# Softmax normalisation moved: attention probabilities multiplied by 1/z on GpSimd ahead of their transposes, in a new order of all mixer operations

## The chip, the core and the metric

The kernel runs on one NeuronCore of a Trainium2 chip. A core has a matrix engine (TensorE, PE in the profile, with its weight loads as PEld), a vector engine (VectorE, DVE), an activation engine (ScalarE, ACT), GpSimd (POOL) and a queue engine (SyncE, SP) that here only starts transfers. The metric is the device time of one execution in microseconds, lower is better.

## What is computed

One layer of an encoder on 512 tokens of width 1024 in float32: a half-step feed-forward network (SwiGLU, inner width 2752), a mixer with two parallel head groups, a second half-step feed-forward network, and a last norm. Cut to what matters here:

```
x = x + 1/2 * SwiGLU_1(RMSNorm(x))
h = RMSNorm(x);  u = h @ w_in            # [ fourier 512 | q 8x64 | k 2x64 | v 2x64 ]
A = FourierMixer(u[:, :512])
q = rope(rms_norm(q)); k = rope(rms_norm(k))
scores = (q . k) / 8                     # each of 8 query heads against its key-value head
p = softmax(scores)                      # exp(s - max) / z,  z = sum of exp over the 512 keys
B = p @ v
x = x + concat([A, B]) @ w_out
x = x + 1/2 * SwiGLU_2(RMSNorm(x))
y = RMSNorm(x)
```

The change concerns the division by z.

## The kernel before

**Tiles and precision.** Activations lie transposed: width on the 128 partitions, the 512 tokens along the free axis. Every product in float32 precision is made of three matmuls on a high part and a low part of each operand (high with high, high with low, low with high). High parts are copies on ScalarE or DVE, low parts are `lows` (line 126, a subtraction on DVE). Weights come from HBM into a raw tile of 512 KB; there are three such tiles (line 89), and a weight's load, its high part and its low part are the operations `.r`, `.h` and `.l`.

**The mixer's operations and their order.** All work of the mixer is cut into named operations. The text `ORDER` (line 47) lists them, and a loop at line 1315 issues them under a manual schedule: each of the five engines executes its own operations in exactly this order, and waits on semaphores for data of the others. Work of the two feed-forward networks on DVE and ScalarE is placed around the mixer's operations by the scheduler at build time; there only PE and SP are in the order of the program (line 120). The names that the prediction uses:

- `wk`, `wq0` to `wq3`, `wv`, `f0` to `f3`, `fw`, `o0` to `o7`: weights; `k.0` to `k.7`, `q0.0` and so on: the eight product steps of a projection.
- `n1.c`, `n1.m`, `n1.p`: the norm ahead of the mixer. `k.sq`, `k.pq`, `k.s0`, `k.s1` (line 900, a power on POOL): the norm of the key heads, likewise for q. `cos`: the loads of the cosine and sine tables. `k.rc`, `k.rs`: the rotation, one and two steps on DVE. `kw`, `kp`, `km`: the keys' norm factors widened, transposed on PE, and multiplied in. `pos`: three tables for the Fourier mixer, loaded from POOL's queue.
- Attention is worked in eight blocks (t, b), t from 0 to 3, b 0 or 1, one query head each. In a block, for each of four groups c of 128 queries: `s` (scores, two matmuls into a PSUM bank, line 1142), `m` (maximum on DVE, line 1148, and its scaling, line 1149), `e` (exponential on ScalarE, which also writes the sum z of its 512 keys). Then for each group kc of 128 keys: `t` (four transposes, one from each of the four query groups, line 1168), `h` and `l` (high and low part), `v` (two matmuls with the values, line 1211, added up over kc). `o..c` and `o..a` collect the two halves of the result.
- `z0.r`, `z0.w`, `z0.p`, `r0.m`: 1/z of both heads of one t, widened to 64 columns on POOL, transposed into rows on PE (line 1200), and multiplied into the collected result (line 1232). `r0.h`, `r0.l` split it for the output projection.
- `map`, `d`, `c`: the Fourier mixer. `y0.0` to `y7.7`: the output projection; `.x` adds the residual, `.h` and `.l` make the operands of the second network's first product, `.q` and `.a` square and accumulate for its norm.

The exponentials lie in a pool of nine tiles (line 763). The eight PSUM banks go around in the order of the list.

**After the mixer** the second network opens with a gate product of eight steps that reads the operands of all eight y; ahead of its last step stand the matmuls for the sums of squares.

Of the kernel before, what the change touches and what calls it, by code (L numbers as in the profile page):

```python
# [6 lines left out]
F32 = mybir.dt.float32  # L7
# [14 lines left out]
HD = 64  # L22
# [30 lines left out]
q1.s1 e001 q2.2 m011 vp q2.3 q1.ah q2.4 s010 f0.r f2.r q1.al q3.1 q2.5 q2.6 e003 q2.7 f0.h q3.2 n1.p m010  # L53
q2.sw s012 q3.3 f0.l f1.h t000 e010 q2.sd e011 q2.rc m012 t003 vs q2.sq h000 fw.r t001 s013 e012 s102 t002
f1.l m102 q3.4 v.h q3.5 h002 q3.6 f00.0 l000 s100 m013 h001 l002 v.l l001 e013 e102 q3.7 q2.pq f2.h m100 v000
q3.sw z0.r q3.sd t010 q2.s0 q1.bh q2.s1 v001 q2.rs f01.0 e100 f2.l s101 f00.1 q2.ah h010 m101 q3.sq f02.0
q1.bl l010 o2.r s103 v002 e101 f02.1 h003 t011 q3.rc q2.bh f00.u l003 h011 m103 q2.bl v003 t013 f02.e e103
t012 o0.r q3.rs q3.pq s112 v010 q3.ah l011 f01.1 q2.al s110 q3.s0 h012 h013 s113 l012 v011 o00.c o00.a l013
m113 m112 s212 e113 m110 f03.0 f01.u e112 m212 q3.al o1.r t103 f03.1 f3.h t101 h101 v012 q3.s1 h103 f03.e
l101 v013 e212 t100 h100 o01.c f10.0 f3.l l103 fw.h s213 l100 q3.bh f12.0 o01.a s111 f03.h f10.1 f02.h q3.bl  # L60
t102 f10.u f03.l e110 s210 s211 h102 v100 m213 z0.w e213 f02.l m111 v101 e111 s201 m210 m211 f12.1 o5.r l102
f12.e e211 z0.p r0.m t111 t112 v102 h111 h112 fw.l l112 v103 o10.c s203 f12.h e210 t110 f11.0 h110 m201 l111
# [6 lines left out]
d3.h c0.l m313 c2.c h300 v202 e313 c1.l v203 y0.0 o20.c m310 h301 l300 c2.o y0.1 e310 d3.l l301 o20.a z2.w
z3.r y1.0 y1.1 c2.h t303 v300 o2.h c3.s c3.c t310 v301 c3.q o7.r t302 c2.l y1.2 h310 h303 c3.o h302 y0.2 l302  # L70
t312 z2.p c3.h v302 c3.l t311 h311 l310 l303 y1.3 y1.4 o6.r z3.w r1.h l311 t313 v310 y0.3 h313 o2.l v303
o30.c r1.l y2.0 y1.5 v311 y2.1 h312 l313 l312 r2.m v312 v313 z3.p o30.a y2.2 y0.4 r2.h o31.c r2.l o31.a y1.6
y0.5 r3.m y0.6 r3.h y2.3 r3.l y0.7 y2.4 o3.h y2.5 y2.6 o3.l y1.7 y2.7 y1.x y3.0 o5.h o5.l y3.1 y3.2 y2.x y0.x
y3.3 y2.q o4.h y5.0 y3.4 o4.l y3.5 y5.1 y0.q y1.q y3.6 y5.2 y5.3 y3.7 y5.4 y5.5 y4.0 y5.6 y4.1 y3.x y4.2 o6.h
# [11 lines left out]
def encoder(ctx, tc, A, out):  # L86
    nc = tc.nc
# [659 lines left out]
    with tc.tile_pool(name="mix", bufs=1) as mp, tc.tile_pool(name="mixt", bufs=1) as mt:  # L747
# [384 lines left out]
        prob, parts, pts, outs, pair, zs, zps, sps, mxs = {}, {}, {}, {}, {}, {}, {}, {}, {}  # L1132
# [50 lines left out]
        def sum_ops(t):  # L1183


            @op(f"z{t}.r")
            def _():
                nc.vector.reciprocal(zs[t], zs[t])

            @op(f"z{t}.w")  # L1190
            def _():
                zw = tp.tile([P, 4, 2, HD], F32, tag="wide", bufs=1, name=f"zw{t}")
                nc.gpsimd.tensor_copy(zw, zs[t].unsqueeze(3).to_broadcast([P, 4, 2, HD]))
                zs[t] = zw

            @op(f"z{t}.p")
            def _():
                zps[t] = bank_for(f"z{t}")
                for c in range(4):
                    nc.tensor.transpose(zps[t][:, c * P : (c + 1) * P], zs[t][:, c].rearrange("p a b -> p (a b)"), ident)  # L1200
# [347 lines left out]
```

## Time and profile before

| | us |
|---|---|
| runs | 824.57, 826.18, 826.47 |
| median of the runs | 826.18 |
| span of the profiled execution, first to last instruction | 821.1 |
| median less span | 5.1 |
| PE busy in the span | 814.0 |
| DVE busy | 640.8 |
| ScalarE busy | 464.5 |
| GpSimd busy | 30.6 |

The profile is of one execution, and gives its span alone; the share of a run ahead of and behind the span is worked out from the median. "L1200" is line 1200 of the kernel. A row "x16" is a group of 16 instructions; in rows of the order in time the first two numbers are start and duration in us, and a bracket gives the idle time before and what ended it. Matmuls overlap: one takes longer from start to end than the distance to the next one's start. TensorE ran at its full granted clock, 1.000.

### The profile page before, as it was taken

Reading aid. Unit: us, or ns where it says so; the run is one execution under the profiler, and the core shown is the slowest. Engines: PE = TensorE matmul, PEld = TensorE weight load, DVE = VectorE, ACT = ScalarE, POOL = GpSimd, SP = SyncE. Lnnn points to the kernel's source line nnn. Section 1 sums busy time; section 2 is a strip of 40 time slices with the busy share of each in tenths; the row PEclk is TensorE's granted clock in tenths of the full one; section 3 lists DMA queues with packets and bytes.
Section 4 is the critical chain, followed back from the end, with each engine's and each line's share of the span. In section 5 each row is a group of like instructions: output and inputs, shape, how many; then the busy total and the mean of one; then the engine's idle time right before and its main releaser. Section 6 shows DMA issues by size and latency. Waiting matters only on the chain.

```text
span 821.1 us, 13621 instructions
## 1 busy us (share of the span) xinstructions
PE 814.0 (99%) x5378; PEld 747.0 (91%) x5378; DVE 640.8 (78%) x996; ACT 464.5 (57%) x777; POOL 30.6 (4%) x34
## 2 busy tenths in 40 slices
PE   9999999999999999999999999999999999999997
PEld 7889999899989998889998888899989999899986
DVE  7998896489756947799998488998945896479574
ACT  7764664167524635676886358556632673256462
POOL 0110000000000000222000000100000000000001
PEclk9999999999999999999999999999999999999999
DMA  7664322323242213621110233552232322322222
GB/s 257 182 145 174 123 91 78 123 103 141 66 153 89 74 58 116 225 77 52 52 52 27 87 105 105 123 170 112 93 121 112 126 103 69 131 104 97 69 78 103
DMA packets 31168, 89.58 MB, mean 109 GB/s; under 512 B 3712, under 2 KB 8832, under 8 KB 31104
## 3 DMA queue, kind: packets, MB, share of 16 engines
q1 hardware_dynamic: 27776, 82.61, 28.9%
q0 software_dynamic: 2608, 5.12, 3.3%
q10 hardware_dynamic: 720, 0.98, 0.3%
q8 instruction: 42, 0.69, 0.3%
q14 instruction: 22, 0.18, 0.1%
HBM read 84.24 MB, written 2.10 MB: 105 GB/s over the span
## 4 chain that ended last, share of the span: by engine, by line
PE 97%; DVE 1%; issue 1%; DMA 0%; ACT 0%; POOLq 0%; POOL 0%; DVEq 0%
PE dn L183 25%; PE r L419 23%; PE q L419 12%; PE mix L183 9%; PE gu L183 8%; PE p L419 6%; PE gu L708 3%; PE mix L1211 2%; PE mix L1168 2%; PE mix L1142 1%; PE mix L1006 1%; PE mix L1008 1%; PE mix L1007 1%; PE mix L1143 1%; PE mix L1065 1%
## 5 line engine op out<-in xcount | busy, mean ns | idle before, releaser
L419 PE MATMUL r<-rt,ring 128*128 128x256 f32 x1686 | 209.3, 276 | 0.0
L183 PE MATMUL dn<-at,ring 128*128 128x512 f32 x900 | 203.3, 380 | 0.5 <-DVE ring L127 0.4
L419 PEld LDWEIGHTS r<-rt,ring 128*128 128x128 f32 x1686 | 200.4, 188 | 0.8
L183 PEld LDWEIGHTS dn<-at,ring 128*128 128x128 f32 x900 | 168.1, 188 | 29.8 <-DVE ring L127 1.6
L419 PE MATMUL q<-rt,ring 128*128 128x256 f32 x840 | 106.6, 276 | 0.0
L127 DVE TENSOR_TENSOR ring<-s,ring 128x1024 fp32r<-128x1024 f32 x70 | 85.6, 1223 | 24.0 <-ACT ring L378 20.8
L419 PEld LDWEIGHTS q<-rt,ring 128*128 128x128 f32 x840 | 100.4, 188 | 0.0
L543 DVE SCALAR_TENSOR_TENSOR gx<-dn,gx 128x512 f32<-128x512 f32 x61 | 42.0, 690 | 67.6 <-PE dn L183 67.6
L378 ACT CAST ring<-s 128x1024 fp32r<-128x1024 f32 x70 | 73.5, 1050 | 28.0 <-PE p L419 13.6
L169 ACT CAST ring<-raw_dn 128x768 fp32r<-128x768 f32 (+3 forms) x58 | 45.2, 783 | 71.1 <-PE dn L183 62.2
L127 DVE TENSOR_TENSOR ring<-raw_dn,ring 128x768 fp32r<-128x768 f32 (+3 forms) x58 | 51.6, 893 | 5.7 <-PE r L419 4.4
L419 PE MATMUL p<-rt,ring 128*128 128x256 f32 x420 | 53.3, 276 | 0.0
L127 DVE TENSOR_TENSOR ring<-raw_g,ring 128x1024 fp32r<-128x1024 f32 x35 | 42.8, 1221 | 11.1 <-PE p L419 10.2
L419 PEld LDWEIGHTS p<-rt,ring 128*128 128x128 f32 x420 | 50.2, 188 | 0.0
L183 PE MATMUL gu<-ring 128*128 128x512 f32 x216 | 48.9, 381 | 0.0
L183 PEld LDWEIGHTS gu<-ring 128*128 128x128 f32 x216 | 40.4, 188 | 6.9
L378 ACT CAST ring<-raw_g 128x1024 fp32r<-128x1024 f32 x35 | 36.8, 1051 | 15.8 <-DMA raw_g<-in_wgu 8.5
L427 ACT COPY p<-r 128x256 f32<-128x256 f32 x35 | 13.0, 371 | 46.8 <-PE r L419 46.5
L451 ACT ACTIVATE g<-g 128x512 f32<-128x512 f32 x35 | 22.1, 633 | 23.4 <-DVE g L450 23.1
L387 ACT CAST ring<-raw_u 128x512 fp32r<-128x512 f32 x35 | 21.8, 624 | 17.4 <-PE q L419 15.9
L183 PE MATMUL mix<-near,ring 128*128 128x512 f32 x120 | 29.7, 383 | 0.0
L464 DVE TENSOR_TENSOR u<-g,u 128x512 f32<-128x512 f32 x35 | 24.1, 689 | 6.1 <-ACT u L463 6.0
(269 smaller groups left out, 1300.5 us busy)
## 6 DMA issues: line engine op xcount, KB each, us to landing
raw_g<-in_wgu SPq DMA_DIRECT2D x35, 512.0 KB, 3.6
raw_u<-in_wgu SPq DMA_DIRECT2D x35, 512.0 KB, 4.4
raw_dn<-in_wd SPq DMA_DIRECT2D x40, 384.0 KB, 3.1
raw_gu<-in_wgu SPq DMA_DIRECT2D x12, 512.0 KB, 3.7
raw_o<-in_wo SPq DMA_DIRECT2D x8, 512.0 KB, 3.5
raw_dn<-in_wd SPq DMA_DIRECT2D x8, 448.0 KB, 3.4
raw_wq<-in_wins SPq DMA_DIRECT2D x4, 512.0 KB, 3.6
raw_f<-in_winf SPq DMA_DIRECT2D x4, 512.0 KB, 4.5
```

The source lines that it names most:

```text
L127: nc.vector.tensor_tensor(out=lo, in0=src, in1=asf(hi), op=ALU.subtract)
L169: nc.scalar.copy(hi[:, :n, :], raw[:, :n, :])
L183: nc.tensor.matmul(ps, a, b, start=first and b is mhi and a is whi, stop=last and a is wlo)
L378: nc.scalar.copy(hi, src)
L387: nc.scalar.copy(hi, src)
L419: nc.tensor.matmul(ps[:, t], a[:, ks], b[:, i, t], start=first and i == 0 and o == 0, stop=i == KH - 1 and o == 2, skip_group_check=not first,
L451: nc.scalar.activation(b["g"], b["g"], AF.Silu)
L464: nc.vector.tensor_tensor(out=u, in0=b["g"], in1=u, op=ALU.mult)
L543: nc.vector.scalar_tensor_tensor(out=x[d][:, t], in0=ps[:, t], scalar=0.5, in1=x[d][:, t], op0=ALU.mult, op1=ALU.add)
L708: nc.tensor.matmul(turned(pss[c]), w[:, k % 2, c], turned(m[k]), start=k == 0 and m is hh and w is hi, stop=k == KD - 1 and w is lo,)
L1168: nc.tensor.transpose(pts[n][:, c * P : (c + 1) * P], prob[t, b, c][:, kc * P : (kc + 1) * P], ident)
L1211: nc.tensor.matmul(turned(outs[t, b]), w, turned(p), start=kc == 0 and i == 0, stop=kc == 3 and i == 1)
```

## The change

1/z is no longer multiplied into the result. `z..` now takes the reciprocal of one head's sums (four per row, of one block), and `p..`, one for each query group, multiplies the 512 probabilities of each query in place by its 1/z on GpSimd. The transposes read the product. The widening on GpSimd, the sixteen transposes of 1/z on PE with their PSUM banks, and the multiplication of the result on DVE are gone. The list of operations is a new one from end to end; of it the parts are shown that the prediction speaks of.

```diff
 ORDER = """
-wq0.r wk.r wv.r wk.h pos wq0.h wk.l k.0 k.1 k.2 k.3 wq1.r k.4 wq1.h k.5 k.6 k.7 wv.h n1.c k.sq wq0.l q0.0
-q0.1 q0.2 cos k.pq wq1.l n1.m q0.3 q0.4 k.sw f3.r q0.5 wv.l wq2.r k.s0 q0.6 k.s1 k.rc q0.7 q1.0 wq2.h k.rs
-q1.1 q1.2 q1.3 q0.rc q0.sq kw f1.r wq2.l kp v.0 q0.sw km k0.2 q0.pq k0.0 k1.0 q0.s0 v.1 q1.4 q0.rs k1.3 q1.5
-v.2 wq3.r k0.1 v.3 q0.bh q1.6 k0.3 q1.7 q2.0 q0.ah q1.sq q0.al s000 v.4 q0.bl v.5 wq3.h s001 s002 s003 q0.s1
-v.6 k1.1 m000 k1.2 q1.sw wq3.l q1.sd q2.1 e000 m002 m003 q1.rc m001 q1.pq e002 v.7 q1.s0 q1.rs vt q3.0 s011
...
-e300 e311 h203 d20 v213 o21.c s303 d21 c0.o h201 l200 t202 v200 o3.r m303 s312 l203 c1.c z2.r e303 o21.a c1.s
-d30 c0.h d2.h l201 c1.q z1.p t300 m312 v201 d2.l c1.o d31 c2.s h202 e312 r1.m s310 l202 s313 c2.q c1.h t301
...
-y1.h y4.3 y2.h y5.7 y4.4 o6.l y4.5 o7.h y5.x y0.h y6.0 y5.h y4.6 y3.h y1.l y1.a o7.l y3.q y6.1 y2.l y5.q y4.7
-y7.0 y4.x y4.q y3.l y7.1 y6.2 y2.a y7.2 y4.h y6.3 y5.l y6.4 y6.5 y3.a y0.l y7.3 y6.6 y6.7 y4.a y5.a y7.4 y6.x
-y4.l y7.5 y6.h y6.l y6.q y7.6 y7.7 y7.x y6.a y7.q y7.h y7.a y7.l
+wk.r wk.h wq0.r wk.l wq0.h k.0 wq1.r wv.r wq2.r wq1.h k.1 k.2 k.3 k.4 k.5 k.6 wq0.l n1.c wq1.l wq3.r k.7 k.sq
+q0.0 n1.m k.sw q0.1 wq2.h k.pq q0.2 cos q0.3 q0.4 q0.5 k.s0 q0.6 k.s1 k.rc k.rs kw q0.7 q1.0 wq2.l wv.h kp q0.sw
+km k1.2 k0.0 k1.0 q0.rc wv.l q1.1 q0.rs q1.2 f1.r q0.ah q2.0 q1.3 q1.4 k0.3 q1.5 k1.3 q0.al q2.1 k0.1 q0.sq q2.2
+k0.2 q2.3 q0.bh q1.6 q1.7 q0.pq wq3.h q1.sq k1.1 q1.sw v.0 s000 v.1 s001 f0.r s002 q0.bl q0.s0 s003 q1.pq wq3.l
+q2.4 q0.s1 q1.rc q2.5 q1.s0 m002 q3.0 m003 s012 q2.6 e003 m000 n1.p m001 q2.7 q3.1 e000 s010 s013 q1.sd q1.rs
+e002 f0.h q3.2 m012 e001 s011 v.2 q1.ah v.3 m010 v.4 f0.l q3.3 z00 m011 q1.al v.5 p001 v.6 q1.bh q2.sw v.7 q2.sq
+q1.bl p000 q2.pq f1.h vt q3.4 p003 e010 p002 m013 vp e011 q3.5 vs s101 t001 q3.6 t003 q1.s1 e012 pos t000 s100
...
+l203 v200 s310 p300 v201 c1.h c2.s m310 v202 c2.q m313 c1.l t300 t302 c2.c e310 h302 e313 y2.0 v203 y2.1 c3.s
+t301 c2.o c3.q h300 o0.l z31 p310 h301 t303 l300 c2.h y0.0 l301 p313 y0.1 v300 l302 c3.c p312 h303 r1.h p311
+c3.o v301 c2.l v302 t310 c3.h h310 o20.c l303 t312 r0.l c3.l r1.l o1.l y0.2 y2.2 t311 h311 v303 h312 y2.3 o30.c
...
+o4.l y0.x y3.2 y3.3 o5.h y3.4 y4.0 y2.x y1.x y1.h y4.1 y0.q y4.2 y3.5 o5.l y3.6 y1.l y0.h y4.3 y3.7 y4.4 y4.5
+o7.h o7.l y0.l y4.6 y5.0 y5.1 y5.2 y1.q y2.q y7.0 y7.1 y3.x y7.2 y5.3 y5.4 y4.7 y5.5 o6.h y2.h y4.x y7.3 y1.a
+y3.q o6.l y5.6 y7.4 y5.7 y2.l y4.q y4.h y2.a y6.0 y7.5 y3.a y7.6 y7.7 y6.1 y6.2 y7.x y4.l y7.h y6.3 y5.x y6.4
+y6.5 y6.6 y3.h y5.h y3.l y5.l y4.a y6.7 y6.x y5.q y7.l y5.a y6.h y6.q y6.l y6.a y7.q y7.a
 """
...
@@ -1129,7 +1129,7 @@
             op(f"c{g}.l")(lambda: lows(ml[g], fos[g, 1], mh[g]))
 
 
-        prob, parts, pts, outs, pair, zs, zps, sps, mxs = {}, {}, {}, {}, {}, {}, {}, {}, {}
+        prob, parts, pts, outs, pair, zs, sps, mxs = {}, {}, {}, {}, {}, {}, {}, {}
 
         def score_ops(t, b, c):
             n = f"{t}{b}{c}"
@@ -1183,21 +1183,18 @@
         def sum_ops(t):
 
 
-            @op(f"z{t}.r")
-            def _():
-                nc.vector.reciprocal(zs[t], zs[t])
-
-            @op(f"z{t}.w")
-            def _():
-                zw = tp.tile([P, 4, 2, HD], F32, tag="wide", bufs=1, name=f"zw{t}")
-                nc.gpsimd.tensor_copy(zw, zs[t].unsqueeze(3).to_broadcast([P, 4, 2, HD]))
-                zs[t] = zw
-
-            @op(f"z{t}.p")
-            def _():
-                zps[t] = bank_for(f"z{t}")
+            for b in range(2):
+
+                @op(f"z{t}{b}")
+                def _(b=b):
+                    nc.vector.reciprocal(zs[t][:, :, b], zs[t][:, :, b])
+
                 for c in range(4):
-                    nc.tensor.transpose(zps[t][:, c * P : (c + 1) * P], zs[t][:, c].rearrange("p a b -> p (a b)"), ident)
+
+                    @op(f"p{t}{b}{c}")
+                    def _(b=b, c=c):
+                        e = prob[t, b, c]
+                        nc.gpsimd.tensor_scalar(out=e, in0=e, scalar1=zs[t][:, c, b : b + 1], scalar2=None, op0=ALU.mult)
 
         def attended_ops(t, b, kc):
             n = f"{t}{b}{kc}"
@@ -1227,11 +1224,6 @@
                 read(f"o{t}{b}")
 
         def result_ops(t):
-            @op(f"r{t}.m")
-            def _():
-                nc.vector.tensor_tensor(out=pair[t], in0=zps[t], in1=pair[t], op=ALU.mult)
-                read(f"z{t}")
-
             op(f"r{t}.h")(lambda: nc.scalar.copy(qa[t], pair[t]))
             op(f"r{t}.l")(lambda: lows(qb[t], pair[t], qa[t]))
 
```

More of the change, by code (lines that the diff above doesn't have):

```diff
@@ L53 @@
[L53 to L62, printed above, removed]
@@ L68 @@
-d30 c0.h d2.h l201 c1.q z1.p t300 m312 v201 d2.l c1.o d31 c2.s h202 e312 r1.m s310 l202 s313 c2.q c1.h t301
[L69 to L72, printed above, removed]
@@ new lines @@
+h113 p213 p210 e201 map1 l113 o4.r m203 e202 v112 f13.e p212 s301 t210 v113 map0 o0.h map1.h d00 e203 t211 m301
+map1.l o11.c e301 d01 o11.a h210 h211 o10.a s302 map0.h l210 f13.h t213 t212 map0.l o6.r d0.h h213 d10 m302 z20
+p200 l211 v210 h212 s303 d11 d0.l s300 l213 c0.s p203 s311 l212 d1.h c0.q p201 e302 p202 v211 d1.l m300 e300
+m303 t201 t202 v212 t200 c0.c m311 f13.l e303 s312 m312 v213 d20 e311 h202 c0.o z30 c1.c h201 r0.h d21 o3.r l201
+d30 c1.s l202 p302 c0.h d2.h h200 c0.l l200 p303 d31 c1.q d3.h o1.h c1.o d2.l s313 d3.l t203 o7.r p301 h203 e312
```

17 lines of the change are left out of this document (11 added, 6 removed).

## The prediction

> **What bounds the kernel now.** I read the page first (busy times, chain), then what TensorE (PE) waited for, then the stretches of the mixer, and last the order in time at three places of it.
>
> ```profile
> span 821.1 us, 13621 instructions
> PE 814.0 (99%) x5378; PEld 747.0 (91%) x5378; DVE 640.8 (78%) x996; ACT 464.5 (57%) x777; POOL 30.6 (4%) x34
> PE 97%; DVE 1%; issue 1%; DMA 0%; ACT 0%; POOLq 0%; POOL 0%; DVEq 0%
> ```
> ```profile
> PE dn L183 <- DVE ring L127: 0.4, 1, 0.4
> 366.00:447.00 81.00, 81.00 (x562) 74.36 (x561) 76.72 (x152) 63.22 (x130) 6.16 (x6) 1.00 0.14 49
> ```
>
> PE is the chain for 97%, its largest wait inside the program is 0.4 us, and that one lies in a feed-forward stage (dn), not in the mixer. The second row of the second fence is the attention stretch, 366 to 447 us, with busy time of PE, weight loads, VectorE (DVE), ScalarE, GpSimd (POOL): PE 81.00 of 81.00, DVE 76.72, POOL 6.16, granted clock 1.00. So the mixer's length is what PE issues. Work that other engines gain or lose costs nothing until PE waits for it. DVE, with 4.3 us free in 81, is the engine that comes next.
>
> **Removed, and what it saves.** Four times: a reciprocal of all eight sums, the widening copy on POOL, four transposes of 1/z, and the multiplication of the result on DVE.
>
> ```profile
> L1200 PE MATMUL mix<-ident,zw x16: 269/272/273, 402.3 to 451.9; 128*128 128x128 f32 x16
> L1188 DVE RECIPROCAL z<-z x4: 182/195/197, 373.6 to 440.2; 128x8 f32<-128x8 f32 x4
> L1232 DVE TENSOR_TENSOR oo<-mix,oo x4: 680/684/691, 403.6 to 453.2; 128x512 f32<-128x512 f32 x4
> L1193 POOL COPY zw<-z x4: 609/614/617, 388.5 to 444.3; 128x512 f32<-128x512 f32 x4
> 344.89 0.60 PE L942 MATMUL mix<-ident,kw 128*128 128x128 f32 x4
> 345.25 0.92 PE L183 MATMUL mix<-ring 128*128 128x512 f32 x3
> ```
>
> A transpose takes 272 ns, but they are pipelined: the next product starts 345.25 - 344.89 = 0.36 us after a set of four began. Four such sets: 1.44 us of PE's issue, and as PE had no idle time in the mixer, all of it is on the path. This is the whole gain that the removal can bring. DVE loses 4 x (0.195 + 0.684) = 3.5 us and gets eight smaller reciprocals, at most 8 x 0.195 = 1.6 us; ScalarE keeps its work. Neither is on the path.
>
> **Added: 32 multiplications on POOL, 128x512, in place.** No row shows one. Nearest rows: the copy above, same shape, 0.61 us; and the two-input multiplication at half the length:
>
> ```profile
> L1334 POOL TENSOR_TENSOR gx<-gx,rb x2: 732/733/734, 810.5 to 811.1; 128x256 f32<-128x256 f32 x2
> ```
>
> Lower bound 0.61; upper bound twice 0.733 = 1.47. The new instruction streams one tensor, like the copy, and has a per-partition factor besides, so I take 0.8. In total 32 x 0.8 = 26 us, which POOL has free; what counts is the time from a block's last score to its first transpose, since a transpose of any 128 keys needs all four products of the block, and 1/z needs all four exponentials.
>
> That time is covered by what the new order gives PE between the two. Prices of PE steps: a full 128x512 product of three matmuls 4.64/21 x 3 = 0.66 (the 21 matmuls below), four transposes 0.36, three 256-column matmuls 0.35, the two matmuls of an attended step 0.54:
>
> ```profile
> 412.45 0.28 PE L1006 MATMUL mix<-ring 128*128 128x256 f32 x1
> 412.80 0.28 PE L1006 MATMUL mix<-ring 128*128 128x256 f32 x1
> 414.20 0.48 PE L1211 MATMUL mix<-ph,near 128*128 128x512 f32 x1
> 414.74 0.40 PE L185 MATMUL mix<-ring,chan 128*128 128x512 f32 x1
> 486.42 4.79 PE L183 MATMUL gu<-ring 128*128 128x512 f32 x21
> 491.06 0.95 PE L241 MATMUL ss<-ones,acc 128*128 128x2 f32 x8
> ```
>
> Counted for all eight blocks, the tightest in the new order is the last, (3,1): between s310 and t310 stand six v, four c, four t and four y steps: 6 x 0.54 + 4 x 0.35 + 4 x 0.36 + 4 x 0.66 = 8.7 us. In the old order the tightest was (3,0): two d halves (six 256-column matmuls each, 0.70), one v, one score (two 512-column matmuls, 0.44), two c, and one set of transposes each for t202 and z1.p: 1.40 + 0.54 + 0.44 + 0.70 + 0.72 = 3.8 us, in which maximum and exponential were done with no wait on PE. That leaves (3,1) 8.7 - 3.8 - 0.2 for the reciprocal = 4.7 us, four multiplications of 1.17 us. But z31 stands on DVE, which executes in order, behind m310, m313, c1.l, c2.o and o0.l:
>
> ```profile
> L1148 DVE TENSOR_REDUCE mx<-mix 128x1 f32<-128x512 f32 x26 | 17.8, 684 | 0.3 <-PE mix L1143 0.2
> L1149 DVE TENSOR_TENSOR mx<-mx,sc 128x1 f32<-128x1 f32 x26 | 4.2, 160 | 1.0
> L127 DVE TENSOR_TENSOR pl<-mix,ph 128x512 fp32r<-128x512 f32 x30 | 20.3, 684 | 1.8 <-ACT ph L1173 1.8
> ```
>
> Two maxima of 0.84, a low of 0.68, c2.o at most like o0.l, a conversion of 1.22, and the reciprocal: 5.0 us, if nothing older is left over. 8.7 - 5.0 = 3.7, a limit of 0.92; an older conversion in the way would make it 0.6. At 0.8 I take the cover to hold: 0 us, and 4 x 0.1 = 0.4 us for every 0.1 us above the limit. The other seven covers, counted in the same way, are 11 us and more, with more score work in them. The multiplications themselves delay on POOL only the head powers of q1 to q3 and n1.p.
>
> **Moved: the constants.** The cosine and sine loads now stand on SP behind wq3, which waits for wq1's raw buffer.
>
> ```profile
> 330.95 0.33 SPq L1291 DMA_DIRECT2D cos<-in_cos  x1
> 331.33 0.43 SPq L1292 DMA_DIRECT2D sin<-in_sin  x1
> 334.22 1.22 DVE L127 TENSOR_TENSOR more<-raw_wq,more 128x1024 fp32r<-128x1024 f32 x1
> cos<-in_cos SPq DMA_DIRECT2D x1, 256.0 KB, 5.0
> raw_fw<-in_fw SPq DMA_DIRECT2D x1, 256.0 KB, 4.3
> 338.48 0.60 PE L889 MATMUL mix<-ident,sq_k 128*128 128x128 f32 x4
> 340.42 0.75 DVE L871 SCALAR_TENSOR_TENSOR rot_k<-mix,qkg,cos 128x512 f32<-128x512 f32 x1 [0.41 <-ACT sw_k L854]
> 342.44 0.75 DVE L871 SCALAR_TENSOR_TENSOR rot_q<-mix,qkg,cos 128x512 f32<-128x512 f32 x1
> 343.11 0.42 DVE L933 TENSOR_SCALAR kw<-sc 128x512 f32<-128x512 f32 x1
> ```
>
> The conversion of wq1 ends at 335.44; then wq3, then cos at about 335.8 (SP steps are 0.38 apart), landing at 340.1 (4.3, as fw) to 340.8 (5.0). k.rc and k.rs take 342.44 - 340.42 = 2.02, kw 0.42, so kw is ready at 342.5 to 343.3. PE reaches kp earlier than before: k.pq goes from third to second place behind q0's products (338.48 - 0.66 = 337.8), and kp follows after 0.36 + 7 x 0.66 = 5.0, at 342.8. Wait 0 to 0.5 us; I take 0.3. The three position tables (POOL's queue) move from the mixer's start to behind the first four multiplications; their first reader is map1, late in the order: 0.
>
> **Moved: the end.** The old order ends with y7, the new one with y6, after more finishing work.
>
> ```profile
> 486.62 0.69 DVE L1254 TENSOR_TENSOR gx<-mix,gx 128x512 f32<-128x512 f32 x1 [0.40 <-PE mix L183]
> 487.23 0.68 DVE L1265 TENSOR_TENSOR acc<-acc,sq 128x512 f32<-128x512 f32 x1
> 487.83 1.22 DVE L127 TENSOR_TENSOR ring<-raw_gu,ring 128x1024 fp32r<-128x1024 f32 x1
> 488.96 1.22 DVE L127 TENSOR_TENSOR at<-raw_gu,at 128x1024 fp32r<-128x1024 f32 x1
> 490.10 0.69 DVE L1265 TENSOR_TENSOR acc<-acc,sq 128x512 f32<-128x512 f32 x1
> 490.70 0.74 DVE L213 SCALAR_TENSOR_TENSOR ring<-gx,ring 128x512 fp32r<-128x512 f32 x1
> ```
>
> The gate product starts at 486.42 and its 21st matmul is followed at 491.06, 4.64 us later, by the sums of squares; the last accumulation ended at 490.79, 0.27 us early. Behind the last product DVE had two operations, two conversions of gate weights that went ahead (1.13 each), then the accumulation. New: y6.x, y7.l, y5.a, y6.l, y6.a, y7.a, with steps of 0.61, 0.69, 0.61, 0.69, 0.61, 0.69: 3.90, from 0.20 behind the last product to 4.10. With both conversions ahead as now: 6.36, so PE waits 1.7 us; with one 0.6; with none 0. I take 1.1, between one and both. What else is late by it: the row of the norm, which follows the sums and moves along with PE.
>
> **Sum.** -1.44 + 0 + 0.3 + 1.1 = 0.0 us on a span of 821.1. The runs' median is 826.18, 5.1 above the span; I leave that share as it is: 826.1. Its own range is 824.7 (both moved places free) to 827.7 (0.5 and 1.7, and 0.8 at the blocks).
>
> **A port of SBUF.** The head powers on POOL, 128x8 each, show that it does not run independently of DVE:
>
> ```profile
> 347.62 2.02 POOL L900 TENSOR_TENSOR sc<-sc,mhalf 128x8 f32<-128x8 f32 x1 [5.85 <-DVE sc L896]
> 348.18 0.69 DVE L878 TENSOR_TENSOR rot_q<-rot_q,sw_q 128x512 f32<-128x512 f32 x1
> 386.87 1.64 POOL L900 TENSOR_TENSOR sc<-sc,mhalf 128x8 f32<-128x8 f32 x1 [9.85 <-DVE sc L896]
> 387.31 0.67 DVE L1226 TENSOR_TENSOR oo<-mix,oo 64x512 f32<-64x512 f32 x1
> ```
>
> Beside a DVE operation with both inputs in SBUF (rot_q, sw_q) the power takes 2.02; beside one with an input from PSUM (mix) 1.64. DVE's 0.69 is not longer there. The Trainium skill, page "SBUF — State Buffer", section "Who interferes with whom", says that the two share a port pair as an exclusive lock, and that whichever comes second waits for the whole instruction; the POOL rows agree in direction, and no row shows DVE waiting. By that rule the sum is that of rival (2).
>
> **Rivals.** (1) All covers hold: -1.44, 824.7. For it: the products that need the two conversions at the end come 5 us later, so these could stand back; against: the rows show both ahead. (2) DVE is held up by POOL: 26 us of multiplications in some 81 are a third of the time. DVE's stretch holds 26 tiny scalings of maxima (two SBUF inputs) and, since maxima (17.8) and lows of PSUM tiles (20.3) make half of the 76.7 us, an estimated 25 other two-input operations among the rest. Of these 51 a third meets a running multiplication and waits half of 0.8: 51/3 x 0.4 = 6.8 us. DVE has 4.3 free plus 1.9 saved. It decides from the point where DVE's loss passes these 6.2 at a block's edge; PE would pay between 0 and 6.8, say 3: 829.1. For it: DVE is 95% busy; against: its rows beside POOL are not longer. (3) The multiplication takes 1.2 us or more: 4 x 0.4 = 1.6 at (3,1), and with three more blocks half exposed 3 x 0.8 = 2.4: 830.1. It decides from about 1.1. (4) More than the transposes goes, over 2.5 us in all: no row of the mixer shows it; 823.6.
>
> **Chances.** Forecast 0.45, (1) 0.2, (2) 0.15, (3) 0.15, (4) 0.05. A difference under 0.3%, 2.5 us, can't be told from none. Faster by more: 0.05, case (4). Slower: (2) and (3), 0.30. Within: 0.65. The range takes in (1) and most of (2) and (3): 824.2 to 829.8.
>
> **What would show it.** No L1200 rows and 32 POOL multiplications near 0.8 us; PE idle before kp up to 0.5 us and before the sums of squares up to 1.7; no wait of a transpose (L1168) for POOL. Rows of two-input DVE operations clearly over 0.69 speak for (2), POOL rows over 1.1 for (3). A time below 823.7 or above 828.7 makes the forecast wrong.

## The result: slower by 1.7%

The changed kernel takes 839.56 us (median of 4 runs, 839.31 to 841.83) beside 826.33 us for the kernel before. The ratio is 1.0171, with a 95% interval of 1.0148 to 1.0195: slower by some 14 us. The forecast of 826.1 us is wrong, and so is its range. (Most kernels' runs lie in two groups about 2.2 us apart, mostly 824 to 825.5 and 826.5 to 828 for the kernel before; the ratios below are of all runs, so where 1 us matters the means of the lower groups are given too, 839.5 for the change and 824.7 for the kernel before.)

The profile after, first the page's head and the chain's line, then PE's waits (in all, times, longest), then the attention stretch with the columns of the prediction:

```profile
span 837.7 us, 13615 instructions
PE 817.4 (98%) x5362; PEld 745.9 (89%) x5362; DVE 640.5 (76%) x996; ACT 464.6 (55%) x777; POOL 79.1 (9%) x62
PE 83%; DVE 8%; POOL 5%; issue 3%; ACT 1%; DMA 0%; DVEq 0%; POOLq 0%
```
```profile
PE mix L1168 <- POOL e L1197: 9.1, 7, 2.4
PE dn L183 <- DVE ring L127: 1.5, 2, 0.9
PE mix L1142 <- ACT e L1156: 1.0, 1, 1.0
PE gu L183 <- DVE ring L213: 0.8, 1, 0.8
...
PE ss L241 <- DVE acc L1257: 0.7, 1, 0.7
```
```profile
366.00:447.00 81.00, 74.25 (x498) 66.70 (x497) 68.58 (x135) 56.93 (x117) 51.65 (x34) 0.98 0.21 68
```

Before, PE was busy for 81.00 of these 81 us and DVE was next with 76.72. Now PE is busy for 74.25 us, POOL for 51.65, and the longest entry among PE's waits is the one that the prediction said would not be there: the transposes of the probabilities (L1168) wait for the multiplications on POOL (L1197). The view of that one line says why (durations in ns: minimum, median, maximum):

```profile
L1197 POOL TENSOR_SCALAR e<-e,z x32: 1554/1567/2399, 365.4 to 454.1; 128x512 f32<-128x512 f32 x32
```

A multiplication takes 1.57 us, not 0.8, and up to 2.4. Four of them, one behind the other, take 6.3 us and more, against a cover that the prediction put at 3.7 us at the tightest block. The timeline at another block, (1,1), shows PE's wait, twice 1.21 us, and the instruction behind each gap:

```profile
404.02 5.15 POOL L1197 TENSOR_SCALAR e<-e,z 128x512 f32<-128x512 f32 x3
...
406.20 0.27 PE L1168 MATMUL mix<-ident,e 128*128 128x128 f32 x1
...
407.68 0.33 PE L1168 MATMUL mix<-ident,e 128*128 128x128 f32 x1 [1.21 <-POOL e L1197]
...
409.22 0.88 PE L1168 MATMUL mix<-ident,e 128*128 128x128 f32 x6 [1.21 <-POOL e L1197]
```

Two more things are in the profile. DVE operations with both inputs in SBUF are longer while POOL multiplies (the grouped rows stand with the experiments). And the wait above is followed by a stretch in which TensorE had half its clock. Four neighbouring windows of 3.41 us (sum of PE, PE's weight loads, DVE, ACT, POOL; granted clock):

```profile
403.26:406.67 3.41, 3.21 (x23) 2.69 (x21) 3.34 (x8) 3.33 (x8) 3.41 (x3) 1.00 0.00 0
406.67:410.08 3.41, 1.19 (x9) 1.00 (x10) 3.30 (x7) 1.89 (x5) 3.41 (x3) 1.00 0.00 0
410.08:413.49 3.41, 3.41 (x17) 3.11 (x16) 0.94 (x3) 0.20 (x1) 2.92 (x3) 0.50 0.02 5
413.49:416.90 3.41, 3.41 (x26) 3.20 (x25) 1.69 (x3) 2.60 (x5) 3.41 (x3) 1.00 0.00 0
```

In the second window PE was busy for 1.19 of 3.41 us. In the third it was busy throughout, at a clock of 0.50, and got through 17 matmuls where the fourth has 26: about half the window, 1.7 us, is lost. So by this estimate a wait of 2.4 us cost some 4 here.

### The profile page after: what moved, and what is told of

Same layout as the page of the kernel before. It is cut to its first block, busy times and chain, and to the rows that moved or that the text cites. A ratio compares the mean times of both kernels' runs of the same rounds, so it can differ in the third digit from the quotient of the medians.

```text
span 837.7 us, 13615 instructions
## 1 busy us (share of the span) xinstructions
PE 817.4 (98%) x5362; PEld 745.9 (89%) x5362; DVE 640.5 (76%) x996; ACT 464.6 (55%) x777; POOL 79.1 (9%) x62
## 4 chain that ended last, share of the span: by engine, by line
PE 83%; DVE 8%; POOL 5%; issue 3%; ACT 1%; DMA 0%; DVEq 0%; POOLq 0%
PE dn L183 24%; PE r L419 23%; PE q L419 11%; PE gu L183 7%; PE mix L183 6%; PE p L419 6%; POOL e L1197 4%; PE gu L708 3%; DVE ring L127 1%; DVE mx L1148 1%; DVE pl L127 1%; PE mix L1168 1%; DVE near L127 1%; DMA raw_first<-in_first 0%; PE last L533 0%
## 5 line engine op out<-in xcount | busy, mean ns | idle before, releaser
L183 PE MATMUL dn<-at,ring 128*128 128x512 f32 x900 | 203.5, 381 | 1.5 <-DVE ring L127 1.5
L183 PEld LDWEIGHTS dn<-at,ring 128*128 128x128 f32 x900 | 168.0, 188 | 31.1 <-DVE ring L127 2.8
L1197 POOL TENSOR_SCALAR e<-e,z 128x512 f32<-128x512 f32 x32 | 51.9, 1637 | 38.9 <-DVE z L1190 38.9
L183 PE MATMUL gu<-ring 128*128 128x512 f32 x216 | 49.2, 382 | 0.8 <-DVE ring L213 0.8
L183 PEld LDWEIGHTS gu<-ring 128*128 128x128 f32 x216 | 40.3, 188 | 8.0 <-DVE ring L213 1.2
L255 POOL TENSOR_TENSOR r<-ms,mhalf 128x4 f32<-128x4 f32 (+1 forms) x4 | 4.3, 1068 | 368.9 <-DVE ms L248 368.9
L900 POOL TENSOR_TENSOR sc<-sc,mhalf 128x8 f32<-128x8 f32 x5 | 9.2, 1847 | 305.4 <-DVE sc L896 305.4
```

Of the source, the lines that this page charges most:

```text
L183: nc.tensor.matmul(ps, a, b, start=first and b is mhi and a is whi, stop=last and a is wlo)
L900: nc.gpsimd.tensor_tensor(out=v, in0=v, in1=mhalf.rearrange("p (c t) -> p c t", t=2), op=ALU.pow)
L1197: nc.gpsimd.tensor_scalar(out=e, in0=e, scalar1=zs[t][:, c, b : b + 1], scalar2=None, op0=ALU.mult)
```

## The experiments

Theories: (A) the price of a multiplication, through the chain of four in front of the transposes; (B) the port, POOL and DVE slowing each other; (C) the new order, whatever normalises. The figures of all kernels first; the ratio is to the kernel before on the same chip, and "no 1/z" means that the result is not divided by the sums.

| kernel | what it is | median us (runs) | ratio [95%] |
|---|---|---|---|
| the change | | 839.56 (4) | 1.0171 [1.0148, 1.0195] |
| e1_no_mult | multiplications out, no 1/z | 826.52 (10) | 1.0016 [1.0003, 1.0028] |
| e2_half | on 256 of 512 columns | 827.6 (10) | 1.0026 [1.0012, 1.0039] |
| e3_pow | chain without streaming, no 1/z | 834.48 (4) | 1.0104 [1.0080, 1.0129] |
| e4_dve | multiplications on DVE | 836.27 (4) | 1.0131 [1.0113, 1.0149] |
| e5_tt | POOL, two-input form | 832.86 (4) | 1.0086 [1.0067, 1.0104] |
| e6_tail | e1, other end, no 1/z | 825.3 (12) | 1.0008 [0.9998, 1.0019] |
| e7_oldz, e13_oldz2 | old normalisation, new order | 830.21 (5), 831.2 (6) | 1.0068 [1.0054, 1.0082], 1.0064 [1.0049, 1.0079] |
| e8_split | half POOL, half ScalarE, end as e6 | 829.49 (5) | 1.0059 [1.0046, 1.0073] |
| e9_stream | streaming without chain, no 1/z | 831.05 (5) | 1.0070 [1.0057, 1.0084] |
| e10_order, e15_order2 | e6, order mended twice, no 1/z | 825.36 (12), 825.3 (12) | 1.0003 [0.9993, 1.0014], 1.0003 [0.9991, 1.0015] |
| e11_mixed | e10, multiplications on three engines | 829.68 (5) | 1.0049 [1.0036, 1.0061] |
| e12_none | old order, no 1/z | 821.9 (6) | 0.9962 [0.9947, 0.9976] |
| e14_oldz3 | old normalisation, new order | 830.24 (6) | 1.0065 [1.0048, 1.0083] |

**Is it the multiplications at all?** e1 takes them out and leaves the order; e2 multiplies half of the columns (the other half is not divided).

```diff
                         e = prob[t, b, c]
-                        nc.gpsimd.tensor_scalar(out=e, in0=e, scalar1=zs[t][:, c, b : b + 1], scalar2=None, op0=ALU.mult)
+                        # e1: nothing here; e2: the same instruction behind  e = e[:, : S // 2]
```

> The new order with the 32 multiplications left out (the result is not divided by z). Theory A (price: the multiplication on GpSimd takes 1.55 us alone, 6.2 us for the four of a block, and PE waits for that at the transposes): the waits of PE at line 1168, 10.4 us, and the stretch of half clock behind two of them, about 1.7 us, go; the waits of the new order that have nothing to do with them, 1.6 us between 352 and 362 us and 1.9 us ahead of the sums of squares, stay: 839.6 - 12.1 = 827.5 us. Theory C (the new order itself is slow, on any engine): 835 us or more.

> Each multiplication on 256 of the 512 columns (the other half of the probabilities is not divided by z), about 0.8 us each, which is the price that the prediction assumed. A: waits at the transposes all but go, 828 us, within 1 us of the kernel without multiplications. If the price is per instruction and not per column, or if the port decides (theory B: GpSimd and DVE hold each other up), the rows stay near 1.5 us and the time stays above 835.

Without them, 13 of the 14 us are gone (1.0171 / 1.0016 = 1.0155, 12.8 us; 14.0 between the lower groups, 839.5 and 825.5). At half the columns an instruction takes 0.93 us, near the forecast's 0.8, and the covers do hold: one wait of 0.4 us for POOL is left on PE, at block (3,1).

```profile
L1198 POOL TENSOR_SCALAR e<-e,z x32: 915/927/1712, 365.3 to 442.6; 128x256 f32<-128x256 f32 x32
PE mix L1168 <- POOL e L1198: 0.4, 1, 0.4
```

So at about the price that the prediction took there is next to no wait. What the covers hold at 1.57 us is another question, answered further down.

**Chain or port?** e3 keeps a chain of the same length without the streaming: in place of each multiplication POOL takes a power of eight columns. e9 keeps the streaming without the chain: the product goes to a tile that nobody reads, and the transposes read the exponentials. Neither divides the result.

```diff
-                        nc.gpsimd.tensor_scalar(out=e, in0=e, scalar1=zs[t][:, c, b : b + 1], scalar2=None, op0=ALU.mult)
+                        # e3 (z: the eight 1/z of the quarter; half: the constant -0.5)
+                        nc.gpsimd.tensor_tensor(out=e[:, :8].rearrange("p (c t) -> p c t", t=2), in0=z, in1=half, op=ALU.pow)
+                        # e9 (o: a tile of its own)
+                        nc.gpsimd.tensor_scalar(out=o, in0=e, scalar1=zs[t][:, c, b : b + 1], scalar2=None, op0=ALU.mult)
```

> Each multiplication replaced by a power of eight columns into the same tile, which takes 1.64 us in the rows of the head norms but streams next to nothing (the result is not divided by z, and eight columns hold other numbers). The chain is as long as with the multiplications, 4 x 1.64 = 6.6 us a block. A: as slow as the change or some 1 to 2 us slower, 840 to 842 us. B (port: streaming against DVE costs the time): the DVE rows with two SBUF inputs are back at 0.69 us, and the time falls to 830 to 833.

> The 32 multiplications run on POOL at the same places with the same operands, but write into a tile that nothing reads; the transposes read the exponentials themselves (so the result is not divided by z). PE never waits for a product, but POOL streams as much as in the change. Chain theory: only the wait for the products costs, so 826.5 us as e1_no_mult. Port theory: the lengthened DVE operations cost by themselves; with the 5 us by which e3_pow (chain without streaming) was faster than the change, 829 to 832 us. In between if DVE's spare time takes up part of it. Rows of DVE with two SBUF inputs should be lengthened (0.93 to 1.07 in place of 0.69) either way.

e3 came out between the theories, e9 at the port theory's 829 to 832. The instructions were the lengths that were wanted, and e9's have nobody waiting for them:

```profile
L1199 POOL TENSOR_TENSOR e<-z,mhalf x32: 1625/1637/2027, 365.2 to 447.6; 128x8 f32<-128x8 f32 x32
PE mix L1168 <- POOL e L1199: 5.1, 3, 2.7
```
```profile
L1198 POOL TENSOR_SCALAR scr<-e,z x32: 1563/1566/2927, 367.6 to 449.9; 128x512 f32<-128x512 f32 x32
```

Over e1, the chain alone costs 1.0104 / 1.0016 = 1.0088, 7.3 us, and the streaming alone 1.0070 / 1.0016 = 1.0054, 4.5 us. Together 11.8 of the 12.8: both theories hold, the chain with the larger part. The profiled executions show where it lies. From the mixer's first product to FFN2's first PE takes 155.8 us in e1, 163.8 in e3, 158.2 in e9 and 168.5 in the change: 8.0 more for the chain (a window of half clock in it), 2.3 for the streaming, 12.7 for both in one. What the streaming does stands in the groups of DVE (360 to 462 us; busy time, mean ns), first e3, then e9:

```profile
L1149 DVE TENSOR_TENSOR mx<-mx,sc 128x1 f32<-128x1 f32 x29 | 4.6, 159 | 3.1 <-POOL sc L900 2.0
L127 DVE TENSOR_TENSOR near<-fe,near 128x512 fp32r<-128x512 f32 x4 | 2.8, 694 | 0.0
L878 DVE TENSOR_TENSOR rot_q<-rot_q,sw_q 128x512 f32<-128x512 f32 x3 | 2.1, 692 | 0.1
```
```profile
L1149 DVE TENSOR_TENSOR mx<-mx,sc 128x1 f32<-128x1 f32 x32 | 6.4, 201 | 3.8 <-POOL sc L900 2.5
L127 DVE TENSOR_TENSOR near<-fe,near 128x512 fp32r<-128x512 f32 x4 | 3.1, 779 | 0.0
L878 DVE TENSOR_TENSOR rot_q<-rot_q,sw_q 128x512 f32<-128x512 f32 x3 | 2.4, 815 | 0.1
```

All three kinds read both inputs from SBUF, and all three are longer on average beside the streaming, though not beside the powers. These sums are small ((201 - 159) x 32 = 1.3 us, 0.3 and 0.3); PE then has small waits for DVE. Whether the rest of e9's cost is the port's is open: its second network, behind the sums of squares, takes 1.3 us more than e1's, with 1.2 us of waits in L183's `dn`, and no multiplication runs there. The change has 1.7 more there, and e10 below, which has no multiplication at all, 1.4; what makes it, no run here separates.

**Is it the form?** The same product as a two-input operation, the second input one column of 1/z repeated.

```diff
+                        z = zs[t][:, c, b : b + 1].to_broadcast([P, S])
-                        nc.gpsimd.tensor_scalar(out=e, in0=e, scalar1=zs[t][:, c, b : b + 1], scalar2=None, op0=ALU.mult)
+                        nc.gpsimd.tensor_tensor(out=e, in0=e, in1=z, op=ALU.mult)
```

> The changed kernel with each POOL multiplication as a two-input operation (TENSOR_TENSOR, 128x512, the second input one column of 1/z repeated) in place of the one-input operation with a factor per partition. Computes the same. Two such operations of 128x256 took 0.733 us each in the profile of before, so 128x512 is at most 1.47 alone, against 1.56 of the one-input form. If the form were dear and the two-input one ran at 1.27 to 1.4, the chain of four shrinks by 0.6 to 1.2 us a block: 834 to 838 us. If POOL needs about 1.5 us for 512 columns whatever multiplies them: 839 to 840, as the change; with rows of DVE lengthened as in the change.

It is the form: 1.04 us in place of 1.57, shorter than either expectation, and the kernel is 7 us faster than the change.

```profile
L1198 POOL TENSOR_TENSOR e<-e,z x32: 1032/1042/1842, 367.9 to 450.3; 128x512 f32<-128x512 f32 x32
PE mix L1168 <- POOL e L1198: 1.5, 2, 0.9
PE mix L1168 <- DVE pl L127: 1.2, 2, 0.9
...
PE mix L1142 <- DVE pl L127: 0.9, 2, 0.7
```
```profile
L1149 DVE TENSOR_TENSOR mx<-mx,sc 128x1 f32<-128x1 f32 x32 | 8.6, 270 | 1.4
L127 DVE TENSOR_TENSOR near<-rot_q,near 64x512 fp32r<-64x512 f32 x6 | 7.0, 1169 | 0.2
366.00:447.00 81.00, 78.22 (x526) 69.55 (x525) 78.75 (x144) 60.45 (x125) 39.37 (x34) 1.00 0.21 68
```

But the port comes forward: the 64x512 lows take 1169 ns on average (686 in e1), the scaling of a maximum 270 (159), DVE is busy for 78.75 of 81 us, and PE waits 2.1 us for lows on DVE. Here the shorter chain came with longer DVE operations; whether the second input or the closer packing of the instructions makes them longer, no run tells.

**Another engine.** e4 puts all on DVE, e8 half of the columns on ScalarE, e11 one of four on POOL, two on ScalarE, one on DVE. e8 has the end of e6 and e11 the order of e10 (below). All three divide by z in full.

```diff
-                        nc.gpsimd.tensor_scalar(out=e, in0=e, scalar1=zs[t][:, c, b : b + 1], scalar2=None, op0=ALU.mult)
+                        nc.vector.tensor_scalar(...)                                   # e4
+                        nc.gpsimd.tensor_scalar(... e[:, :256] ...)                    # e8
+                        nc.scalar.activation(e[:, 256:], e[:, 256:], AF.Copy, scale=z)
+                        how = spread.setdefault((t, b), ["pool", "act", "act", "dve"]).pop(0)   # e11
```

> The same 32 multiplications on DVE instead of GpSimd, in the same places of the order. A cast of 128x1024 between two SBUF tiles takes 0.69 us on DVE, so 128x512 should take about 0.36: 11.5 us more on an engine with 4.3 us free of 81 before. A: the chain of a block shortens from 6.2 to 1.5 us, but DVE is over its share by some 6 us: 832 to 834 us. If DVE takes 0.69 each: 22 us, 843 or more.

> Each multiplication is split: 256 columns on POOL (0.8 us alone), 256 on ScalarE, with the last products in the order of e6_tail. Price theory: the POOL chain is halved as in e2_half (1.1 us over e1_no_mult), ScalarE has 24 us free in the 81 of the attention stretch and takes 32 x about 0.35 = 11, and the tail gives 1.9 back: 825.5 to 827 us. Rival: ScalarE executes in order and its exponentials and copies stand behind multiplications that wait for 1/z, so PE waits for ScalarE instead: 830 us or more.

> e10_order with the multiplications in it, shared out: of the four of a block the first runs on POOL (1.56 us alone), two on ScalarE (an activation of 128x512 takes 0.7), one on DVE (0.48), side by side, so a block's chain is about 1.6 us in place of 6.3. It computes what the reference computes. Chain theory: the covers of the order (3.7 us and more) hold all chains; DVE gets 3.8 us in the mixer, of which it has 6 free, and meets 8 in place of 32 POOL multiplications: 0 to 1.5 us over e10_order, 822.5 to 824.5, no slower than the kernel before. Rival: ScalarE and DVE execute in order, and what they have to do besides is late instead: 826 or more, as e4_dve (all on DVE, 836) suggests.

On DVE a product takes 478 ns (0.36 us was expected), the shortest chain of the kernels on one engine, and the kernel is still 1.3% slower: DVE was the engine that comes next.

```profile
L1197 DVE TENSOR_SCALAR e<-e,z x32: 468/478/493, 367.1 to 450.9; 128x512 f32<-128x512 f32 x32
366.00:447.00 81.00, 76.41 (x510) 66.94 (x509) 78.83 (x168) 57.64 (x120) 3.86 (x2) 1.00 0.15 50
```

Sharing out is better (e8 1.0059, e11 1.0049), but slower than expected and than the kernel before: small waits for each of the three engines remain. No kernel here beats the kernel before with the division in it.

**The order.** e6 moves y5's and y7's finishing work ahead of the last product y6.7; e10 exchanges y6 and y7 and starts q0's sums and powers earlier; e15 does the end and q0's powers as the kernel before does. All on e1, so without division. e12 is the kernel before with its normalisation left out.

```diff
-y4.a y6.7 y6.x y5.q y7.l y5.a y6.h y6.q y6.l y6.a y7.q y7.a
+y4.a y5.q y7.l y5.a y7.q y7.a y6.7 y6.x y6.h y6.q y6.l y6.a        (e6)
+y4.a y5.q y6.l y5.a y6.q y6.a y7.7 y7.x y7.h y7.q y7.l y7.a        (e10; e15: ... y7.x y7.q y7.h y7.a y7.l)
-q0.bl q0.s0 s003 q1.pq wq3.l q2.4 q0.s1 q1.rc q2.5 q1.s0 m002 q3.0 m003
+q0.bl s003 q1.pq wq3.l q2.4 m002 q1.rc q2.5 q1.s0 q3.0 m003        (e10; q0.s0 q0.s1 stand behind q0.pq)
```

> The kernel of e1_no_mult (the multiplications of p are left out, so the result is not divided by z) with the last products in another order: y4.a y5.q y7.l y5.a y7.q y7.a now stand ahead of y6.7 and y6.x. Behind the last product DVE has then only y6.x, y6.l and y6.a to do. The forecast's head term says that what DVE does behind the last product is what PE waits for at the FFN2 head: in e1_no_mult 0.96 + 0.11 + 0.85 = 1.9 us there, now about 0, so 826.5 - 1.9 = 824.6 us. Rival: the conversions of the gate weights are what is late, whatever stands around them: then the waits stay, 826.5 us.

> The kernel of e6_tail (no multiplications, the result not divided by z) with two more places of the order mended: y6 and y7 (and their weights) change places, so that what is finished last is the chunk that FFN2's first products read last; and q0's sums and powers (q0.s0, q0.s1) stand right behind their transposes, with m002 ahead of q1.rc and q1.s0. Theory: the remaining waits of the order are these two, 1.27 us at the FFN2 head and 1.85 us between the first scores (352 to 362 us), so e6_tail less 2.5 to 3.1: 822.2 to 822.9 us, and below the kernel before by about the 1.44 us of the 16 transposes left out. Rival: the time is lost at other places of the order, or the waits move on: 824.5 or more.

> e10_order (no multiplications, the result not divided by z) with the two places done as the kernel before has them: q0.sq directly behind q0.sw, q0.pq, q0.s0 and q0.s1 behind q1.2, so q0's powers are ready some 4 us earlier; and at the end y7.x y7.q y7.h y7.a y7.l, so the accumulation of squares goes ahead of the low part. If these two places are the order's cost, the waits of 1.3 us before the sums of squares and 1.3 us at the scores (357.4 and 360.5) vanish: 825.3 - 2.6 = 822.7, near e12_none (821.9). If not, the 3.6 us of the order are spread over other places, and the time stays near 825.

> The kernel before, in its own order, with its normalisation left out (reciprocals, widening copies, 16 transposes and the four multiplications of the result; the result is not divided by z). It measures the term of the forecast by which the change could gain at most: 16 transposes, 4 x 0.36 = 1.44 us, so 824.5 - 1.4 = 823.1 us on the same chip, 0.17% below the kernel before. Rival: more hangs on them than PE's issue (the results of r.m come 0.7 us later on DVE, ahead of y0.4 to y0.7): 822 or less. Together with e6_tail and e10_order, which leave the same work out in the new order, it tells what the new order costs.

The waits move rather than go. The first row is e6's (there the last low part is late, where e1 had 0.8 and 0.7), the second e10's (now the accumulation), the last two e15's (half of it is left, and q0.pq, early, waits for its squares):

```profile
PE gu L183 <- DVE ring L213: 1.0, 1, 1.0
...
PE ss L241 <- DVE acc L1256: 1.1, 1, 1.1
...
PE mix L889 <- ACT sq_q L841: 1.8, 1, 1.8
PE ss L241 <- DVE acc L1256: 0.5, 1, 0.5
```

e6 brought about 0.5 us of the 1.9 expected, e10 and e15 nothing more. The old order without division is another matter: 821.9 us, 3.1 us below the kernel before (ratio interval 2.0 to 4.4 us), and none of these waits. So without any division the new order costs 1.0016 / 0.9962 = 1.0054, 4.5 us; the lower groups give 3.5, and the profiled executions 3.7. In these it can be placed: the mixer, from its first product to FFN2's first, is 153.99 us in e12 and 155.81 in e1, and from FFN2's first product to the sums of squares it is 4.63 and 6.54. So the cost lies at the two places that the trace names, the first scores and the head of FFN2; e10 and e15 keep most of it (156.04 and 156.82 us, 5.94 and 5.28), with the waits of the rows above.

**The order in a whole kernel.** The old normalisation fitted into the new order (z.r and z.w behind the last sums, z.p and r.m ahead of their readers). In e7 and e13 the conversion o3.h stood ahead of y2.7 and replaced a weight that y2.7 still reads; the instructions are the same. In e13 and e14 each z.w from the second on stands behind the transposes of the quarter before, which e7's overwrites.

```diff
-... p001 ... p000 ... z01 ... (32 p, 8 z)
+... z0.r z0.w ... z0.p r0.m f13.0 ... z1.p r1.m r1.h ... z2.p y2.5 ... z3.p y1.3 ... r2.m y0.5 r2.h ... r3.m r3.h
```

> The changed kernel with the old normalisation put back: four reciprocals, four widening copies on POOL, 16 transposes of 1/z and four multiplications of the result, the transposes well behind the copies; all else in the new order (beside a few steps of y1 to y3 that change places to cover the later results). It tells the price of the order alone. If the order costs what e1_no_mult showed on top of the 1.44 us of transposes (waits of about 2 us at the scores and 1.9 at the FFN2 head), it takes 826.5 + 1.4 = 828 us. Rival: the order is bad only together with multiplications on POOL; then it takes 826.2, as the kernel before. In both cases nearly all of the 14 us belongs to the multiplications, and a time of 832 or more would refute that.

> e7_oldz with each widening copy (z1.w, z2.w, z3.w) behind the transposes of the quarter before, so that it doesn't overwrite factors that are still to be read: it computes what the reference computes, and is the new order with the old normalisation. e7_oldz less its slow start: if only the order costs, e1_no_mult (825.5 to 826.5) plus 1.44 for the transposes plus 0.8 for two waits that the results' later places made in e7_oldz: 827.7 to 829. Rival, the order is no worse than the old one with the old normalisation: 824.5 to 825.5.

> e13_oldz2 with o3.h behind y2.7: in e7_oldz and e13_oldz2 the conversion of output weight 3 stood ahead of y2.7 and replaced a weight that y2.7 still read. This one computes what the reference computes; all work of the kernel before, in the order of the change (the old normalisation fitted in). The order alone: e1_no_mult minus e12_none is 825.5 - 821.9 = 3.6 us of order without any normalisation; with the old normalisation on top, 825.4 + 3.6 = 829 us, and e13_oldz2 says up to 831. Rival: 825.4, the order costs nothing with the old normalisation.

All three agree: the order alone makes the kernel 0.65% slower, 5.4 us (4.0 to 6.9; 4.6 between the lower groups; in e14's profiled execution 3.3 in the mixer and 1.9 at the head of FFN2), with the waits of e1 at the scores and the FFN2 head, and a few of 0.3 to 0.4 us at the fitted places, which are mine and not the change's.

## Why the prediction was wrong

**The price of the multiplication** is the step that failed: "I take 0.8", between 0.61 and 1.47. It measured 1.57 alone, above the upper end. The bounds were rows of other forms, the copy and a two-input operation, and the argument that the new one "streams one tensor, like the copy" put it near the wrong end. The two-input form, as e5 shows, is 1.04 at this size; the one-input form with a factor per partition was dearer than both neighbours. No row of the trace before showed that form at this shape on POOL; a range that stops at twice a neighbour was not a bound. With 1.57, the limit of 0.92 at block (3,1) fails by 0.65 x 4 = 2.6 us; the trace shows 2.60 more than usual there (453.0) and 1.06 to 1.43 at six other transposes, 10.4 us from start to start (9.1 as idle time in the table of waits), and the half clock on top.

**The covers** are the second step that failed, and at 0.8 us it did not show. "The other seven covers ... are 11 us and more" is right from a block's last score: e1's trace has 11.1 to 20.2 us there, and 8.4 at (3,1). But the multiplications start at 1/z, and only for (3,1) did the prediction subtract what DVE has to do before. At (2,0) the last score ended at 412.7, and 1/z came 9 us later:

```profile
421.85 0.17 DVE L1190 RECIPROCAL z<-z 128x4 f32<-128x4 f32 x1
...
425.63 0.60 PE L1168 MATMUL mix<-ident,e 128*128 128x128 f32 x4
```

From the end of 1/z to the first transpose, e1 has 3.1 us at (3,1) (the prediction had 3.7), 3.6 at (2,0), 4.6 at (1,1), 5.3 at (3,0), 5.7 at (0,0), and 7.5 to 8.8 at the other three. Four multiplications are 3.2 us at the price taken, 3.7 in e2 and 6.3 in the change: in e2 (3,1) alone waits, in the change the five blocks below 6.3, and no other. That the 2.6 us reckoned for (3,1) met the 2.60 measured is partly luck: in e1 that cover is 3.1 us, and only in the change, with waits ahead of it, 3.7.

**Rival (3)** had the mechanism, its point of decision (about 1.1) and its place; its 830.1 was for 1.2 us. e5, at a mean of 1.17, is 1.0086 / 1.0016 = 1.0070, 5.8 us over e1, against the rival's 4.0, the port's part in it. Its price was too low for the change: it had three more blocks exposed, and four were.

**Rival (2)** is real too. The prediction set against it that DVE's rows beside POOL were not longer. One of its two rows (L1226) reads an input from PSUM; the other (L878) has both inputs in SBUF, but stood beside a power of eight columns, which, as e3 shows (692 ns), lengthens nothing. Beside a multiplication the same operation is 0.37 us longer than the 0.69 of before:

```profile
380.40 3.63 POOL L1197 TENSOR_SCALAR e<-e,z 128x512 f32<-128x512 f32 x2
...
381.08 1.06 DVE L878 TENSOR_TENSOR rot_q<-rot_q,sw_q 128x512 f32<-128x512 f32 x1
```

Its price was about right: 3 us at PE above the sum, measured 4.5 by e9's runs, 2.3 of it in the mixer. The Trainium skill, "SBUF — State Buffer", "Who interferes with whom", names this pair, a DVE instruction with two SBUF inputs and a GpSimd instruction that reads SBUF, and the rows agree in who is hit. The whole-instruction wait, which the prediction took from it, the page states for DVE's two-port modes; the rows here don't show it: 0.37 us was added beside an instruction of 1.57, and POOL's own were longer too (up to 2.4).

**The removal** was taken at 1.44 us by PE's issue. It is worth 3.1 (e12; 2.8 between the lower groups). The mixer, from its first product to FFN2's first, is 155.67 us before and 153.99 in e12, 1.68 less, near the 1.44; another 0.47 lies outside the span (2.27 us in the runs of the kernels with the old normalisation, e14 among them, 1.80 in those without). The rest is within what the runs tell apart. (The 5.1 us that the prediction left outside the span were mostly the distance between two executions: with 2.27 outside, the profiled one took some 823.4.)

**The cosine and sine loads** were given 0.3 us. The step was right on DVE and wrong on PE: in e1 k.rc waited for cos, and the trace has no idle time of PE ahead of kp, in e1 or in the change; PE came to kp at 343.55 in e1, 0.75 us later than reckoned.

```profile
340.70 0.75 DVE L871 SCALAR_TENSOR_TENSOR rot_k<-mix,qkg,cos 128x512 f32<-128x512 f32 x1 [0.96 <-DMA cos<-in_cos]
```

**The end** was given 1.1 us; e1's trace has 0.96 + 0.11 + 0.85 = 1.9 more than usual there (6.54 us from FFN2's first product to the sums of squares, 4.63 before), above the 1.7 for "both conversions ahead". Both were, and FFN2 reads y6 ahead of y7, so y6's low part, the last but one, was late first. That reader's order was not in the prediction.

**What it left out:** the wait at the first scores. The sum of q0's squares stands behind lows of k and q on DVE, its power on POOL is ready at 357.25, the first exponential starts at 360.21, and a score waits for the bank that it frees. Of the 2.96 us between, 1.28 are ScalarE's load of a table ahead of its first exponential; the kernel before has the same load at 354.16, early enough that no score waits. With smaller ones the wait is 1.6 to 1.8 us in all. The prediction counted covers from the scores on, not the path to the first. From the timeline after:

```profile
354.69 2.56 POOL L900 TENSOR_TENSOR sc<-sc,mhalf 128x8 f32<-128x8 f32 x1 [13.06 <-DVE sc L896]
...
358.92 1.28 ACT L1156 ACT_TABLE_LOAD   x1 [4.32 <-DVE mx L1149]
...
360.21 0.78 ACT L1156 ACTIVATE e<-mix,mx,sc 128x512 f32<-128x512 f32 x1
...
361.13 0.49 PE L1142 MATMUL mix<-ks,near 128*128 128x512 f32 x1 [0.95 <-ACT e L1156]
```

The ledger in us. Each row is the difference of two kernels, so the rows add up to the whole by construction, and the sum checks nothing; the columns do check each other.

| step | forecast | by the ratios | lower groups | mixer | head of FFN2 |
|---|---|---|---|---|---|
| removal (before to e12) | -1.4 | -3.1 | -2.8 | -1.7 | 0.0 |
| order (e12 to e1) | +1.4 | +4.5 | +3.5 | +1.8 | +1.9 |
| multiplications (e1 to the change) | 0 | +12.8 | +14.0 | +12.7 | 0.0 |

The last two columns are of one profiled execution each: the mixer from its first product to FFN2's first, and from there to the sums of squares.

## What to carry to other kernels

A price for an instruction that the trace doesn't show is bounded by rows of its own form, not of its shape; without one, the range has to reach to where the covers break, and here one test at full size (or the two-input form) would have settled it. A cover counts from where the last input of the chain is ready, here 1/z, and not from PE's last step ahead of it. A chain of four on a slow engine in front of PE costs up to four times what one link is over its limit, and a cover that holds says nothing about what the same instructions do to the engine beside it. The gain of leaving work out and the cost of the order that this needs are measured apart: here the order alone ate more than the whole removal could bring.

## What the hardware showed that I had not expected

The forms on POOL, all f32: a copy of 128x512 0.61 us, a two-input multiplication 1.04, a multiplication by a factor per partition 1.57, at 256 columns 0.93; so (1.57 - 0.93) / 256 = 2.5 ns a column for the last form, about (1.04 - 0.73) / 256 = 1.2 for the two-input one.

TensorE's clock fell to half for 3.41 us not only behind idle time but behind windows of 3.41 us in which PE was busy for part of the time: 35% in the change, 41% and 57% in e3, which paid it twice, 57% in e4. But the share of busy time, as the profile has it, does not decide it. In e15 a window with 47% was followed by the full clock, and in the change one with 55% (430.57); in e2 one with 75%, at the head of FFN2, was followed by half the clock. First e15, then e2:

```profile
347.09:350.50 3.41, 1.59 (x10) 1.10 (x9) 1.08 (x2) 3.36 (x6) 0.00 (x0) 1.00 0.47 154
350.50:353.91 3.41, 3.41 (x18) 2.89 (x16) 3.34 (x6) 1.86 (x4) 0.39 (x1) 1.00 0.44 132
```
```profile
492.25:495.66 3.41, 2.55 (x14) 2.04 (x15) 1.57 (x4) 0.20 (x1) 0.50 (x1) 1.00 0.76 263
495.67:499.08 3.41, 3.41 (x9) 2.55 (x9) 1.38 (x3) 3.02 (x4) 0.53 (x1) 0.50 0.07 13
```

In e1 no stretch of the mixer has it. The Trainium skill, "TensorE: Matmul & The Clock Gate", section "What's actually happening", gives a free-running window of 3413 ns, and says that the clock falls after an idle window. The length is seen here (e3's two stretches of 3.41 us began 51.2 us apart, 15 windows). None of the windows above was idle, and what decides between them stays open. So this time comes and goes: e1 and e2 have the same two waits at the head of FFN2, 0.8 and 0.7 us, only e2's execution fell to half the clock there, and from its sums of squares to the last product of the network it took 308.45 us, e1's 307.08.
